# Trainium2: a decoder block's start, its third attention dilation, one split of gate weights and the first merge

## The chip, the cores and the metric

The kernel runs on one core of one Trainium2 chip. Its engines are TensorE (PE in the profile; PEld is its weight load), VectorE (DVE), ScalarE (ACT), GpSimd (POOL) and SyncE (SP), which here only issues DMAs. The metric is the device time of one execution in microseconds, the median of several. The arithmetic is fp32, kept by products of three: each operand is split into a high part (rounded to the type fp32r) and a low part, and high x high, high x low and low x high are summed in PSUM.

## The reference

For 2048 tokens of width 1024:

```python
h = rmsnorm(x, norm_pre_mix)
proj = h @ w_in                      # 1024 x 5376
q, k = rope(proj[:, :768]), rope(proj[:, 768:1536]); v = proj[:, 1536:2304]
u, z = gelu(proj[:, 2304:2816]), gelu(proj[:, 2816:3328])
gate_a, gate_b = sigmoid(proj[:, 3328:4352]), sigmoid(proj[:, 4352:])
y_attn = attention(q, k, v)          # 12 heads of 64 in 3 groups; dilations 1, 4, 16, window of 129 keys
y_gmlp = u * (tril(w_spatial) @ layernorm(z) + b_spatial)     # per chunk of 128 tokens
y = (gate_a * (y_attn @ w_branch_attn) + gate_b * (y_gmlp @ w_branch_gmlp)) @ w_out
x = x + rmsnorm(y, norm_post_mix)
h = rmsnorm(x, norm_pre_mlp)
x = x + rmsnorm(relu(h @ w_mlp_in) ** 2 @ w_mlp_out, norm_post_mlp)
```

A token t of a dilation d belongs to residue t mod d; within a residue the attention is a plain causal band, worked in blocks of 128.

## The kernel before

The kernel runs in stages over four chunks (c = 0 to 3) of 512 tokens, each of four blocks of 128.

*Values, queries, keys.* A block of x is loaded (`load_x`), normalised with the gain `gpre` (`prenorm_rows`), transposed by TensorE and split into `hT` (`prenorm_cols`, which also keeps a copy `hr` for DRAM, `hTd`). `v_block` multiplies it by the value weights: `va` for dilations 1 and 4, `vb` for the third. The weights of the first blocks, raws 0 to 2, are loaded by `early_load` and split on several engines by `early_split`. Six fp32 matmuls on a tile of ones (`busy`) stand ahead. `qk_pair` then projects queries and keys, rotates them (`t1`, `t2` on VectorE, `r` on POOL, L287 to L293), and stores high and low parts in DRAM (`qk_d`). For the dilations 4 and 16 the rotation's last step also reorders the tokens: for 4, by residue. For 16, `r` holds four groups of residues, and in a group (length index, residue) stand interleaved, so that a residue's elements are four apart.

*Attention and gates.* An attention unit handles one head and 512 tokens: loads of `kp` and `qq` (L546, L551) two units ahead, scores (L580 for the third dilation, L583 and L584 for the others), softmax on VectorE and ScalarE, transposes (L627), the value products (L646), and a sum `o` on VectorE (L653). Between its steps TensorE computes other columns of the projection: `filler` runs through u, z and the 16 pairs of gate columns, whose weights `w_g` are loaded one ahead by `load_w`: two raw halves, high parts on POOL (L72), low parts on VectorE or POOL (L78). When its first half of tokens is done, `reload_h` fetches `hT` of the other chunks from DRAM and splits it on POOL. The gates go to DRAM (`gate_d`).

*Merge.* For each chunk, in the order 2, 3, 0, 1, and for each of eight blocks of columns dt, `merge` loads two gates, takes their sigmoid on ScalarE, multiplies them by the branch products (L813), adds (L815) and splits the sum for the product with w_out. Meanwhile, in the first merge, `spatial_out` works off the last spatial products and loads and splits one eighth of w_out (`load_wo`) per dt. `out_block` multiplies by w_out, normalises, adds x and normalises again for the MLP. After that come the MLP's two products, which the change doesn't touch.

*What sets the order.* TensorE runs in the order of the program text. The instructions of the other engines and of SyncE's queue are put in order by a planner that follows the data; inside `as_written()` those too run in the order of the text, and `behind()` makes later ones follow the last one so far. Every engine runs its list in order: a waiting instruction holds up the ones behind it.

## Time and profile before

| | |
|---|---|
| median of 3 runs | 2757.62 us (2757.6 to 2757.78) |
| the profiled execution's own time | 2753.64 us |
| its span | 2751.9 us |
| mean granted TensorE clock | 0.994 |
| TensorE busy | 2699.0 us, 98% |
| VectorE, ScalarE, POOL busy | 57%, 38%, 35% |
| DMA moved | 426.00 MB, 155 GB/s |

A row of the timeline has the start and the length in us, the engine, the line, the operation, out<-in and the count; in brackets stands the idle time ahead of it and what ended that. In a row of a group stand the count, the busy time in us and the mean in ns of one. TensorE's matmuls are pipelined, so the distance between two starts is shorter than one's length.

### The profile page before, as it was taken

How to read it: one execution, taken by the hardware profiler on the slowest of the kernel's cores; microseconds unless marked ns; L12 is line 12 of the kernel's file. 1: busy time of each engine (PE TensorE's matmuls, PEld its weight loads, DVE VectorE, ACT ScalarE, POOL GpSimd, SP SyncE). 2: the span in 40 equal slices, each digit the busy share in tenths (PEclk: the TensorE clock that was granted, in tenths of full speed). 3: DMA queues.
4: the chain of work that ended last, by engine and by line, in shares of the span. 5: the costliest groups of instructions: out<-in, count | busy, mean ns of one | idle time of the engine just before them, and what ended most of it. 6: DMA issues, size and time to landing. Idle time of an engine off the chain costs nothing. (4 is left out here: it accounts for less than half of the span.)

```text
span 2751.9 us, 34711 instructions
## 1 busy us (share of the span) xinstructions
PE 2699.0 (98%) x12668; PEld 2237.4 (81%) x12668; DVE 1558.8 (57%) x2646; ACT 1050.3 (38%) x2145; POOL 965.5 (35%) x782
## 2 busy tenths in 40 slices
PE   8999999999999999999999999999999999999998
PEld 7888888888888888787787788878887888888887
DVE  5655552344343345555556644655436878888866
ACT  5213111244444322344444544555544332233334
POOL 0351341200140013302215432223214766676645
PEclk9999999999999999999999999999999999999999
DMA  7445446366676645555658433554343122222236
GB/s 266 171 146 172 153 143 211 112 195 196 192 222 200 194 159 176 184 191 161 184 168 287 154 106 124 181 171 119 111 138 122 52 87 85 84 85 85 87 107 213
DMA packets 298380, 426.00 MB, mean 155 GB/s; under 512 B 18528, under 2 KB 172384, under 8 KB 298208
## 3 DMA queue, kind: packets, MB, share of 16 engines
q1 hardware_dynamic: 206672, 370.28, 41.6%
q10 hardware_dynamic: 91536, 53.49, 6.5%
q8 instruction: 100, 1.64, 0.2%
q14 instruction: 72, 0.59, 0.1%
HBM read 282.99 MB, written 140.71 MB: 154 GB/s over the span
## 5 line engine op out<-in xcount | busy, mean ns | idle before, releaser
L1558 PE MATMUL ya<-T_spots,s 128*128 128x512 f32 x1176 | 291.6, 391 | 3.3 <-DVE acc L1566 3.3
L1558 PEld LDWEIGHTS ya<-T_spots,s 128*128 128x128 f32 x1176 | 220.7, 188 | 52.3 <-ACT T_spots L70 3.1
L70 ACT ACTIVATE s<-sraw 128x768 fp32r<-128x768 f32 (+1 forms) x184 | 127.4, 696 | 337.5 <-POOL sraw L1355 150.0
L1016 PE MATMUL aa<-B,A 128*128 128x512 f32 x768 | 186.9, 395 | 8.5 <-ACT xs L1030 7.7
L78 DVE TENSOR_TENSOR s<-sraw,s 128x512 fp32r<-128x512 f32 x171 | 179.6, 1075 | 7.1 <-ACT s L70 7.0
L987 POOL TENSOR_TENSOR s<-w1r 128x512 f32<-128x512 f32 x32 | 42.3, 1322 | 396.6 <-DVE S L78 337.9
L1016 PEld LDWEIGHTS aa<-B,A 128*128 128x128 f32 x768 | 145.0, 190 | 43.1 <-ACT xs L1030 9.0
L1558 PE MATMUL yc<-T_spots,s 128*128 128x512 f32 x624 | 160.8, 391 | 0.0
L72 POOL TENSOR_SCALAR w_g<-w_g_r 128x1024 fp32r<-128x1024 f32 x32 | 34.1, 1081 | 354.3 <-PE g L97 292.8
L95 PE MATMUL x<-hT_a,wq 128*128 128x512 f32 x384 | 149.7, 390 | 0.0
L97 PE MATMUL x<-hT_a,wq 128*128 128x512 f32 x384 | 149.5, 389 | 0.0
L96 PE MATMUL x<-hT_a,wq 128*128 128x512 f32 x384 | 149.4, 389 | 0.0
L653 DVE TENSOR_REDUCE o<-po 128x256 f32<-128x512 f32 x48 | 33.1, 690 | 194.4 <-PE po L652 194.4
L1558 PEld LDWEIGHTS yc<-T_spots,s 128*128 128x128 f32 x624 | 117.2, 188 | 25.6
L70 ACT ACTIVATE hl<-r 128x512 fp32r<-128x512 f32 x48 | 30.4, 633 | 233.2 <-POOL r L287 89.0
L78 POOL TENSOR_TENSOR T_spots<-w2r,T_spots 128x512 fp32r<-128x512 f32 x70 | 104.6, 1521 | 7.5 <-ACT T_spots L70 7.5
L95 PE MATMUL o<-wo,mg 128*128 128x512 f32 x256 | 101.5, 396 | 5.1 <-ACT mg L70 4.6
L95 PE MATMUL g<-hT_b,w_g 128*128 128x512 f32 x256 | 105.6, 412 | 0.0
L815 POOL TENSOR_TENSOR g<-g,g 128x512 f32<-128x512 f32 x28 | 38.8, 1385 | 187.4 <-DVE g L813 187.2
L95 PE MATMUL g<-hT_a,w_g 128*128 128x512 f32 x256 | 104.3, 407 | 0.0
L1354 POOL TENSOR_TENSOR sraw<-sraw 128x256 f32<-128x256 f32 x56 | 41.4, 739 | 178.4 <-DVE s L78 164.1
L70 ACT ACTIVATE S<-w1r 128x512 fp32r<-128x512 f32 x96 | 60.0, 629 | 114.2 <-PE ac L1016 69.3
(380 smaller groups left out, 7272.2 us busy)
## 6 DMA issues: line engine op xcount, KB each, us to landing
w1r<-in_w_mlp_in_dram SPq DMA_DIRECT2D x64, 512.0 KB, 3.5
sraw<-sd SPq DMA_DIRECT2D x128, 256.0 KB, 3.4
qk<-hl SPq DMA_DIRECT2D x24, 1024.0 KB, 5.3
qq<-qk SPq DMA_DIRECT2D x96, 256.0 KB, 5.0
w_g_r<-in_w_in_dram SPq DMA_DIRECT2D x32, 512.0 KB, 5.0
gated<-gt SPq DMA_DIRECT2D x64, 256.0 KB, 3.3
g<-gated SPq DMA_DIRECT2D x64, 256.0 KB, 4.3
sd<-u ACTq DMA_DIRECT2D x64, 256.0 KB, 2.8
```

Of the source, the lines that this page charges most:

```text
L70: act.activation(hi, src, AF.Copy)
L72: pool.tensor_scalar(hi, src, 1.0, 1.0, op0=OP.mult, op1=OP.mult)
L78: (pool if lo_eng == "pool" else dve).tensor_sub(lo, src, f32(hi))
L95: pe.matmul(ps, lh, rh, start=start, stop=False)
L96: pe.matmul(ps, lh, rl, start=False, stop=False)
L97: pe.matmul(ps, ll, rh, start=False, stop=stop)
L653: dve.tensor_reduce(ot[:, :, j * 64:(j + 1) * 64], po.rearrange("p (b h e) -> p b e h", b=4, h=2), axis=AX.X, op=OP.add)
L815: (dve if dt == KT - 1 else pool).tensor_add(parts[0], parts[0], parts[1])
L987: pool.tensor_add(s1, a21, a22)
L1016: pe.matmul(p, w[:, l, k, :], h[:, r, k, :], start=i in (1, 6, 5) and not k and not n, stop=k == 3 and n == 2, skip_group_check=True)
L1354: pool.tensor_add(a22, a21, a22)
L1558: pe.matmul(p, s[:, l], w[r], start=i in (1, 2, 5) and not m and not o, stop=m == 1 and o == 2, skip_group_check=True)
```

## The change

Four things change.

1. *Start.* The gain row (4 KB) is loaded to one partition of a zeroed tile and spread to 128 partitions by two fp32 matmuls with ones, into two PSUM banks from which the first block is normalised; ScalarE copies them to `gpre` later. Before, one DMA spread it (512 KB). There are five busy matmuls ahead of the spread and two behind. The high parts of the first weights are all ScalarE's and the low parts all VectorE's, in the order of the text, with the copies `hr` of the first block last.
2. *First merge.* `early_gates` asks for eleven gates ahead of the merge, six in places that are used later by `xr`, `gpost` and `gmlp`, with the first two w_out loads between; w_out is loaded two eighths ahead. All adds L815 are VectorE's. In the other merges the loads of the next `yt` stand behind the first out block.
3. *Third dilation.* The rotation writes each residue contiguously, `kp` is loaded as four pieces (one residue each, four runs of 32 elements per row), and the product reads queries of a residue contiguously and keys in runs of 32.
4. *Gate weights.* With half 0, POOL takes the low parts of the third weight in place of those of the first two.

On VectorE at the start, where `raw_126`, `raw_127`, `raw_128` are the three weight raws, before:

```order
L192 SCALAR_TENSOR_TENSOR x_122<-x_122,r_pre_146,gpre 128x512 x2
L78 TENSOR_TENSOR wv_1_130<-raw_126,wv_1_130 128x4x256
L78 TENSOR_TENSOR wv_0_129<-raw_126,wv_0_129 128x4x256
L206 TENSOR_TENSOR hT_a_161<-pt_162,hT_a_161 128x4x128
L206 TENSOR_TENSOR hT_a_161<-pt_172,hT_a_161 128x4x128
L189 TENSOR_TENSOR ss_182<-ss_182 128x1
```

and in the changed kernel, with raws 130 to 132:

```order
L203 SCALAR_TENSOR_TENSOR x_127<-x_127,r_pre_152,gpre_124 128x512
L385 TENSOR_TENSOR wv_0_133<-raw_130,wv_0_133 128x4x256
L218 TENSOR_TENSOR hT_a_169<-pt_170,hT_a_169 128x4x128
L218 TENSOR_TENSOR hT_a_169<-pt_177,hT_a_169 128x4x128
L385 TENSOR_TENSOR wv_1_134<-raw_130,wv_1_134 128x4x256
L385 TENSOR_TENSOR wv_0_133<-raw_131,wv_0_133 128x4x256
L385 TENSOR_TENSOR wv_1_134<-raw_131,wv_1_134 128x4x256
L200 TENSOR_TENSOR ss_191<-ss_191 128x1
```

One low part now stands behind the split of `hT`, and both of the second raw stand ahead of the second block's normalisation.

ScalarE a little later, where `x_308` is the third block, before:

```order
L205 ACTIVATE hT_a_161<-pt_269 128x4x128
L188 ACTIVATE junk_311,ss_310<-x_308 128x512
L188 ACTIVATE junk_313,ss_310<-x_308 128x512
L209 ACTIVATE hr_266<-pt_259 128x512
L209 ACTIVATE hr_276<-pt_269 128x512
L102 ACTIVATE r_pre_316<-ss_310,edge 128x1
L322 ACTIVATE vt_208<-vb_210 128x4x64
```

and now, where it is `x_320`:

```order
L342 ACTIVATE vt_220<-va_221 128x8x64
L199 ACTIVATE junk_323,ss_322<-x_320 128x512
L199 ACTIVATE junk_325,ss_322<-x_320 128x512
L229 ACTIVATE hr_278<-pt_271 128x512
L229 ACTIVATE hr_288<-pt_281 128x512
L342 ACTIVATE vt_220<-vb_222 128x4x64
L102 ACTIVATE r_pre_328<-ss_322,edge 128x1
```

The root for the third block has moved behind the copy of `vb`.

SyncE's queue at the first merge (`g_20` is a gate of chunk 2, dt 0), before:

```order
L91 DMA yt_9506<-ygd 128x512
L795 DMA g_20_9526<-gated 128x512
L795 DMA g_20_9537<-gated 128x512
L91 DMA woraw_9601<-in_w_out_dram 128x1024
L795 DMA g_21_9605<-gated 128x512
L795 DMA g_21_9616<-gated 128x512
```

and now:

```order
L863 DMA gates_9583<-gated 128x512 x2
L839 DMA woraw_9588<-in_w_out_dram 128x1024
L863 DMA gates_9584<-gated 128x512 x2
L839 DMA woraw_9592<-in_w_out_dram 128x1024
L863 DMA gates_9585<-gated 128x512 x2
L872 DMA g_23_9596<-gated 128x512
L872 DMA g_23_9598<-gated 128x512
```

The loads are the same; the gates stand further ahead of their use.

POOL at the third gate weight of half 0 (`w_g_6903`, now `w_g_6915`), before:

```order
L72 TENSOR_SCALAR w_g_6903<-w_g_r_6904 128x1024
L72 TENSOR_SCALAR w_g_6903<-w_g_r_6908 128x1024
L72 TENSOR_SCALAR hT_b_6538<-hT_b_6538 128x1024
L78 TENSOR_TENSOR hT_b_6538<-hT_b_6538 128x1024
L72 TENSOR_SCALAR hT_b_6538<-hT_b_6538 128x1024
```

and now:

```order
L72 TENSOR_SCALAR w_g_6915<-w_g_r_6916 128x1024
L72 TENSOR_SCALAR w_g_6915<-w_g_r_6920 128x1024
L78 TENSOR_TENSOR w_g_6915<-w_g_r_6916,w_g_6915 128x1024
L78 TENSOR_TENSOR w_g_6915<-w_g_r_6920,w_g_6915 128x1024
L72 TENSOR_SCALAR hT_b_6550<-hT_b_6550 128x1024
```

Two low parts now stand between the high parts and the split of `hT_b`.

The diff, cut:

```diff
-    def prenorm_rows(c, i):
+    def prenorm_rows(c, i, gs=None):
...
-        for sl in cuts(c, i):
-            dve.scalar_tensor_tensor(xt[:, sl], xt[:, sl], r, gpre[:, sl], op0=OP.mult, op1=OP.mult)
+        for n, sl in enumerate(cuts(c, i)):
+            dve.scalar_tensor_tensor(xt[:, sl], xt[:, sl], r, gs[n] if gs else gpre[:, sl], op0=OP.mult, op1=OP.mult)
...
+            kept.append((k, p3))
+            if (c, i) != (0, 0):
+                keep_cols(c, i, kept)
+        return kept
+    def keep_cols(c, i, kept):
+        while kept:
+            k, p3 = kept.pop(0)
...
-                pool.tensor_tensor(r.rearrange("p (m l r) -> p m l r", m=4, r=4),
-                                   t1.rearrange("p (l m r) -> p m l r", m=4, r=4),
-                                   t2.rearrange("p (l m r) -> p m l r", m=4, r=4), op=op)
+                pool.tensor_tensor(r.rearrange("p (m r l) -> p m r l", m=4, r=4),
+                                   t1.rearrange("p (l m r) -> p m r l", m=4, r=4),
+                                   t2.rearrange("p (l m r) -> p m r l", m=4, r=4), op=op)
...
-        act.dma_start(gpre, bcast(a["norm_pre_mix"]))
+        rp = stack(e1a, "rp", 1, side="right")
+        row = rp.tile([P, D], F32, name="row", tag="rope", bufs=2)
+        busy = rp.tile([P, 256], F32, name="busy", tag="t1", bufs=2)
+        pool.memset(row, 0.0)
+        dve.memset(busy, 1.0)
-        rp = stack(e1a, "rp", 1, side="right")
-        busy = rp.tile([P, 256], F32, name="busy", tag="t1", bufs=2)
-        dve.memset(busy, 1.0)
+        act.dma_start(row[0:1], a["norm_pre_mix"])
+        act.dma_start(ident, a["ident"])
+        p = psum_aux("busy")
+        for _ in range(5):
+            pe.matmul(p[:, :256], busy[:, :P], busy, start=True, stop=True)
+        gp = [psum_mm(f"gpre{n}") for n in range(2)]
-            p = psum_aux(f"busy{n}")
-            for _ in range(3):
-                pe.matmul(p[:, :256], busy[:, :P], busy, start=True, stop=True)
+            pe.matmul(gp[n], busy[:, :P], row[:, n * 512:(n + 1) * 512], start=True, stop=True)
         load_x(0, 0)
-        sp.dma_start(ident, a["ident"])
         raws = [rp.tile([P, 2, 4, 256], F32, name=f"raw{g}", tag=t, bufs=2) for g, t in enumerate(("hl", "hl", "vt"))]
                 sp.dma_start(raws[g][:, kk], w_src(6 + g, kk))
-        def early_split(g, *engs):
-            for kk in range(2):
-                w = part(wide0[kk], g) if g < 2 else third0[:, kk]
-                split(w[:, 0], w[:, 1], raws[g][:, kk], *engs[kk])
-        early_load(0)
-        load_x(0, 1)
-        early_load(1)
-        early_load(2)
-        prenorm_rows(0, 0)
-        early_split(0, ("pool", "dve"), ("act", "dve"))
-        prenorm_cols(0, 0)
-        prenorm_rows(0, 1)
-        early_split(1, ("act", "pool"), ("act", "dve"))
-        early_split(2, ("act", "dve"), ("pool", "dve"))
+        def early(g, kk):
+            w = part(wide0[kk], g) if g < 2 else third0[:, kk]
+            return w[:, 0], w[:, 1], raws[g][:, kk]
+        def hi(g, kk):
+            w = early(g, kk)
+            act.activation(w[0], w[2], AF.Copy)
+        def lo(g, kk, eng):
+            w = early(g, kk)
+            eng.tensor_sub(w[1], w[2], f32(w[0]))
+        with as_written():
+            early_load(0)
+            load_x(0, 1)
+            early_load(1)
+            early_load(2)
+            prenorm_rows(0, 0, gp)
+            p = psum_aux("busy")
+            for _ in range(2):
+                pe.matmul(p[:, :256], busy[:, :P], busy, start=True, stop=True)
+            hi(0, 0)
+            hi(0, 1)
+            lo(0, 0, dve)
+            kept = prenorm_cols(0, 0)
+            lo(0, 1, dve)
+            hi(1, 0)
+            hi(1, 1)
+            lo(1, 0, dve)
+            lo(1, 1, dve)
+            for n in range(2):
+                act.activation(gpre[:, n * 512:(n + 1) * 512], gp[n], AF.Copy)
+            prenorm_rows(0, 1)
+            hi(2, 0)
+            hi(2, 1)
+            lo(2, 0, dve)
+            lo(2, 1, dve)
+            keep_cols(0, 0, kept)
+        first = behind()
...
-                loaded[q] = load_w(wi, f"w_{kind}{n}{half}", "pool" if (kind, half) == ("g", 0) and n < 2 else "dve")
+                loaded[q] = load_w(wi, f"w_{kind}{n}{half}", "pool" if (kind, half) == ("g", 0) and n == 2 else "dve")
...
-        sp.dma_start(f32(kp)[:, :nkb * P], qk_d[g][one][j * P:(j + 1) * P, k0:k0 + nkb * P])
+        rows = qk_d[g][one][j * P:(j + 1) * P, k0:k0 + nkb * P]
+        if g == 2:
+            for r in range(4):
+                sp.dma_start(f32(kp)[:, r * P:(r + 1) * P].rearrange("p (c l) -> p c l", c=4),
+                             rows.rearrange("p (c r l) -> p r c l", c=4, r=4)[:, r])
+        else:
+            sp.dma_start(f32(kp)[:, :nkb * P], rows)
...
-                    pe.matmul(o.rearrange("p (h k) -> p h k", h=2), kp[:, b:512:4], qq[:, :, b::4],
-                              start=True, stop=True)
+                    pe.matmul(o.rearrange("p (h c l) -> p h c l", h=2, c=4), kp[:, b * P:(b + 1) * P],
+                              qq.rearrange("p h (c r l) -> p r h c l", c=4, r=4)[:, b], start=True, stop=True)
...
+    wo_raw = {}
     def load_wo(k):
-        raw = bot.tile([P, D], F32, name=f"woraw{k}", tag="y1", bufs=2)
-        split_in(wo[k], a["w_out"][:, k, :], raw, "act")
+        wo_raw[k] = bot.tile([P, D], F32, name=f"woraw{k}", tag="y1", bufs=2)
+        sp.dma_start(wo_raw[k], a["w_out"][:, k, :])
+    def split_wo(k):
+        split(wo[k][:, 0], wo[k][:, 1], wo_raw.pop(k))
+        if k + 2 < KT:
+            load_wo(k + 2)
...
+    def early_gates(c):
+        w = [bot.tile([P, D], F32, name=f"gates{n}", tag=t) for n, t in enumerate(("xr", "gpost", "gmlp"))]
+        places = [z[:, h * 512:(h + 1) * 512] for z in w for h in range(2)]
+        for n in range(11):
+            dt, wch = n // 2, n % 2
+            if n < 6:
+                gates[c, dt, wch] = places[n]
+                sp.dma_start(places[n], gate_d[wch * 8 + dt, :, c * 512:(c + 1) * 512])
+            else:
+                load_gate(c, dt, wch)
+            if n in (1, 3):
+                load_wo(n // 2)
...
-            (dve if dt == KT - 1 else pool).tensor_add(parts[0], parts[0], parts[1])
+            dve.tensor_add(parts[0], parts[0], parts[1])
...
-        load_wo(dt)
+        split_wo(dt)
...
+    early_gates(2)
...
-        if n < 3:
-            yt = load_y(chunks[n + 1])
-            for dt in range(2):
-                for wch in range(2):
-                    load_gate(chunks[n + 1], dt, wch)
...
+            if n < 3 and not i:
+                yt = load_y(chunks[n + 1])
+                for dt in range(2):
+                    for wch in range(2):
+                        load_gate(chunks[n + 1], dt, wch)
```

More of the change, by code (lines that the diff above doesn't have):

```diff
@@ L164, in block_kernel, with as_written, behind @@
     st = stack(e1, "st", 2)
+    def as_written():
+        t = mybir.EngineType
+        return tc.manual_schedule(engines={t.Activation, t.DVE, t.Pool, t.SP})
+    def behind():
+        es, t = ExitStack(), mybir.EngineType
+        for e in (t.Activation, t.DVE, t.Pool, t.SP):
+            es.enter_context(tc.issue_after(next(i for i in reversed(nc.cur_bb.bb.instructions) if i.engine == e)))
+        return es
     hT = {}
@@ L198, in prenorm_cols @@
         h, xt = hT[c], xts.pop((c, i))
+        kept = []
         for k in range(0, KT, 4):
@@ L380, in block_kernel @@
                 v_block(rp, wv, c, i, between)
+                if (c, i) == (0, 1):
+                    first.close()
             nxt = load_w(0, f"wq00{half}")
@@ L771, in block_kernel @@
     sm = stack(e2b, "sm2", 2)
[L772 to L773 removed]
+    gpost = gmlp = None
     gtp = stack(e2, "gtp", 2)
@@ L1088, in spatial_out @@
     def spatial_out(dt):
-        nonlocal ttp
+        nonlocal ttp, gpost, gmlp
         if dt < 2:
@@ L1096, in spatial_out @@
             ttp = stack(e2r, "ttp", 2, side="right")
-        load_wo(dt)
+        split_wo(dt)
         if dt == KT - 1:
+            gpost = bot.tile([P, D], F32, name="gpost")
+            gmlp = bot.tile([P, D], F32, name="gmlp")
             sp.dma_start(gpost, bcast(a["norm_post_mix"]))
@@ L1140, in block_kernel @@
                     lone_a(1, q, n_, raw.rearrange("p (k c) -> p k c", k=4))
-    def as_written():
-        t = mybir.EngineType
-        return tc.manual_schedule(engines={t.Activation, t.DVE, t.Pool, t.SP})
-    def behind():
-        es, t = ExitStack(), mybir.EngineType
-        for e in (t.Activation, t.DVE, t.Pool, t.SP):
-            es.enter_context(tc.issue_after(next(i for i in reversed(nc.cur_bb.bb.instructions) if i.engine == e)))
-        return es
     first_half, second_half = 1, 0
```

2 lines of the change are left out of this document (removed).

## The prediction

> **What bounds the kernel.** I read the page's first part, then TensorE's waits grouped by releaser, then the timeline at each of them. In a row of the waits stand the total, the count and the longest, in us.
>
> ```profile
> span 2751.9 us, 34711 instructions
> PE 2699.0 (98%) x12668; PEld 2237.4 (81%) x12668; DVE 1558.8 (57%) x2646; ACT 1050.3 (38%) x2145; POOL 965.5 (35%) x782
> ```
> ```profile
> ...
> PE b L95 <- DVE g L813: 5.0, 4, 1.7
> PE o L95 <- ACT mg L70: 4.6, 4, 1.9
> PE pT L627 <- DVE o L653: 4.1, 2, 3.4
> ...
> PE pt L868 <- DVE y L862: 3.4, 1, 3.4
> ```
>
> TensorE is busy for 98% of the span, so time is saved only where it stands still or where a busy matmul is slower than it need be. The second kind isn't in the list of waits. The sum below is made against the profiled execution's 2753.64 us (span 2751.9); the median of the runs is 2757.62, 4.0 more, so I add 4.0 at the end. What can be told from no change is 0.2%, 5.5 us.
>
> **A, the start.**
>
> ```profile
> 1.31 5.46 PE L339 MATMUL busy<-busy 128*128 128x256 f32 x12 [1.31 <-DVE busy L335]
> 10.32 1.94 PE L202 MATMUL pt<-ident,x 128*128 128x128 f32 x8 [3.55 <-DVE x L192]
> ...
> 15.81 0.42 PE L96 MATMUL va<-wv,hT_a 128*128 128x256 f32 x1
> ...
> 17.11 0.28 PE L97 MATMUL va<-wv,hT_a 128*128 128x256 f32 x1
> ...
> 21.09 0.39 PE L96 MATMUL va<-wv,hT_a 128*128 128x256 f32 x1 [1.43 <-DVE wv L78]
> ...
> 26.26 0.40 PE L95 MATMUL va<-wv,hT_a 128*128 128x512 f32 x1
> ```
> ```profile
> 6.61 0.60 ACT L188 ACTIVATE junk<-x 128x512 f32<-128x512 f32 x1 [0.71 <-DMA x<-in_x_dram]
> ```
> ```profile
> 8.72 2.16 DVE L192 SCALAR_TENSOR_TENSOR x<-x,r_pre,gpre 128x512 f32<-128x512 f32 x2
> 10.93 2.36 DVE L78 TENSOR_TENSOR wv<-raw,wv 128x1024 fp32r<-128x1024 f32 x2
> ```
> ```profile
> 15.14 2.42 POOL L78 TENSOR_TENSOR wv<-raw,wv 128x1024 fp32r<-128x1024 f32 x1 [5.46 <-ACT wv L70]
> ```
>
> (Start, length, engine, line; in brackets the idle time before and what ended it.) The busy matmuls end at 6.77, the first transposes come at 10.32, and va's matmuls take 0.42 us at 15.81 and 0.28 at 17.11: the clock was half until then. VectorE's normalisation at 8.72 goes back to ScalarE's second square at 6.61, which waited for x's DMA. The change takes 512 KB (gpre spread to 128 rows) out of the queues ahead of x, so I let x land 1 to 2 us earlier and the normalisation start at about 7.1. Two matmuls that spread the gain and two more busy ones fill TensorE until then (two passes each of 5.46/12 = 0.455 us, more for the 512 wide ones: to about 8.9), so the clock stays up. Then va's 48 matmuls run at the short length, and group 1 no longer stands behind POOL's 2.42 us low part (VectorE's is 2.36/2 = 1.18): the 1.43 at 21.09 goes too. I put group 1's end near 16.8 and vb's near 22.2, where va of the next block begins at 26.26 now: 4 us. Part is given back. In ScalarE's new order the third block's r_pre stands behind vb's copy (before, ahead of it), so that block's transposes come an estimated 1.4 us late. I take 2.5, with 0 to 4 as ends: nothing if x's landing isn't set by gpre. POOL's memset of the row (128x1024) and two gain copies on ScalarE are new; ScalarE's idle time there covers the copies, the memset runs beside x's load.
>
> **B, the first merge, and the adds.**
>
> ```profile
> 1119.45 0.80 SPq L795 DMA_DIRECT2D g<-gated  x2
> ```
> ```profile
> 1125.83 1.28 DVE L813 TENSOR_TENSOR g<-g,b 128x512 f32<-128x512 f32 x2 [1.21 <-ACT g L809]
> 1175.16 0.69 DVE L815 TENSOR_TENSOR g<-g,g 128x512 f32<-128x512 f32 x1
> ```
> ```profile
> 850.00:900.00 50.00, 49.93 (x260) 42.94 (x260) 20.05 (x78) 19.71 (x67) 2.07 (x2) 1.00 0.69 214
> 900.00:950.00 50.00, 50.00 (x264) 43.24 (x263) 18.81 (x65) 17.59 (x57) 4.12 (x4) 1.00 0.60 185
> 950.00:1000.00 50.00, 50.00 (x262) 42.96 (x262) 14.92 (x63) 18.34 (x58) 2.06 (x2) 1.00 0.32 108
> ...
> 1119.30:1168.10 48.80, 42.50 (x209) 33.54 (x207) 33.04 (x50) 22.11 (x32) 15.16 (x10) 1.00 0.76 235
> ```
> ```profile
> L815 POOL TENSOR_TENSOR g<-g,g 128x512 f32<-128x512 f32 x28 | 38.8, 1385 | 187.4 <-DVE g L813 187.2 <-DVE r_pm L105 0.2
> ```
>
> The third of these fences is the busy time of stretches: from and to, length, then PE, weight loads, VectorE, ScalarE, POOL, the granted clock, DMA's share and GB/s. In the last stretch, the first merge's products, TensorE stands still for 48.80 - 42.50 = 6.3 us at full clock, most of it the 5.0 on the gates; about 1.4 of the 4.6 on the last parts (L95 o) follow in the out block behind it: 7.7. The first gate isn't asked for until 1119.45, and from then on gate, sigmoid, product, POOL's add (1.385 us) and ScalarE's and VectorE's split run as a chain through two or three buffers. In the change two gates are asked for ahead of that time and nine right at it, and the add takes 0.69 on VectorE in place of 1.385 plus a handover. What is late next is VectorE: it is busy for 33.0 us of the stretch, seven more adds make it 33.0 + 7 x 0.69 = 37.8, and the stretch shrinks towards 42.5, so its queue holds up a product here and there. I let 1 of the 7.7 stay and take 6.7, ends 3 (VectorE sets the pace) and 7.7. On SyncE the first wo load waits for a place that z's products read until 1119, as the first gate did, and holds nine gates behind it; at 0.40 an issue (0.80 for two) all are out within 5 us. The cover is the two gates ahead of it, which feed the first product.
>
> The later merges' adds also move: 24 x (1.385 - 0.69) off their chains, 0.69 more on VectorE each. Their longest stall, 3.4 at y (L862), has two adds and a split ahead of it on VectorE, with less beside them on POOL. I take nothing, with 1.5 either way. Moving the loads of yt behind the first out block leaves them hidden under that block's products.
>
> **C, the third dilation.**
>
> ```profile
> L580 PE MATMUL s<-qq,kp 128*128 128x256 f32 x64 | 20.6, 460 | 0.0
> ```
> ```profile
> 742.29 0.29 PE L583 MATMUL s<-kp,qq 128*128 128x256 f32 x1
> 742.42 0.28 PE L584 MATMUL s<-kp,qq 128*128 128x256 f32 x1
> ...
> 849.55 1.29 PE L580 MATMUL s<-qq,kp 128*128 128x256 f32 x4
> 850.66 0.41 PE L95 MATMUL g<-hT_b,w_g 128*128 128x512 f32 x1
> 859.23 1.29 PE L580 MATMUL s<-qq,kp 128*128 128x256 f32 x4
> ```
> ```profile
> q1 hardware_dynamic: 206672, 370.28, 41.6%
> q10 hardware_dynamic: 91536, 53.49, 6.5%
> ```
> ```profile
> 842.71 0.58 SPq L546 DMA_DIRECT2D kp<-qk  x1
> ```
> ```profile
> L289 POOL TENSOR_TENSOR r<-t,t 128x512 f32<-128x512 f32 x16 | 36.2, 2273 | 19.2 <-DVE t L284 19.2
> L293 POOL TENSOR_TENSOR r<-t,t 128x512 f32<-128x512 f32 x16 | 22.3, 1406 | 22.9 <-DVE t L284 19.3 <-DVE ss L189 3.6
> ```
>
> At L580 queries and keys are read at every fourth element, and a matmul takes 460 ns; one of the same shape on contiguous operands (742.29, an earlier dilation) takes 280 to 290. Four of L580 hold TensorE from 849.55 to 850.66, 1.11 us; the contiguous ones come 0.13 apart, 0.52 for four. TensorE is full in those stretches (49.93 and 50.00 of 50), so each of 16 units is 0.59 shorter: 9.5 us.
>
> The price is kp's load: 128 runs of 2 KB become 2048 of 128 bytes, in four DMAs. From the page's queues a q10 packet of 584 bytes took 6.5% x 16 x 2751.9 / 91536 = 31 ns and a q1 packet of 1792 bytes 89. The line through both gives 9 ns at 128 bytes; no gain from being smaller gives 31. A unit now takes 9.68 us (849.55 to 859.23), its DMA work 0.69 x 9.68 = 6.7, and 2.4 us are free in the new 9.1. kp's packets take 128 x t per engine against about 0.8 now: at 20 ns, between the ends, 1.8 more, which is hidden; at 31 ns 3.2 more, which costs 0.8 in each of the five units of the first window and nothing in the later ones (0.60): 4 us. SyncE's issue grows from 0.58 to 2.3 of 9 us. The rotation before it (L293) now gathers with a step of 16 elements: 1.4 us becomes at least the 2.27 of L289's four-step gather, 16 x 0.87 = 14 us on POOL, under TensorE's projections, which never wait for it (no row in the list). I take 9, ends 4 and 10.
>
> **D, the gate weights' low parts.**
>
> ```profile
> 784.98 0.48 PE L627 MATMUL pT<-ident,e 128*128 128x128 f32 x1 [3.44 <-DVE o L653]
> ...
> 786.53 0.63 PE L97 MATMUL g<-hT_b,w_g 128*128 128x512 f32 x1
> ...
> 788.24 0.40 PE L95 MATMUL g<-hT_b,w_g 128*128 128x512 f32 x1
> ```
> ```profile
> 780.29 4.04 DVE L78 TENSOR_TENSOR w_g<-w_g_r,w_g 128x1024 fp32r<-128x1024 f32 x2 [4.79 <-POOL w_g L72]
> ```
> ```profile
> 745.99 4.76 POOL L78 TENSOR_TENSOR w_g<-w_g_r,w_g 128x1024 fp32r<-128x1024 f32 x2
> ```
>
> VectorE's low parts of the third gate weight, slowed beside POOL's work to 4.04 for two, run to 784.3 and hold up the reduction behind them (L653), and with it TensorE's transposes: 3.44, and then matmuls of 0.63 until 788.24, where 0.40 is usual. From 784.98 on that is 3.3 us at half pace, 1.6 lost. Both go: 5.0. The two weights before it come to VectorE without POOL beside them (2.36 for two, as at 10.93); an attention step behind them can wait for that, up to 0.5 each. On POOL the third weight's 4.76 now stands ahead of the second half of hT_b's splits; I put their results level with TensorE's need, so a stall of up to 1 can come there. I take 4.5, ends 2.5 and 5.0.
>
> **Sum.** 2.5 + 6.7 + 9 + 4.5 = 22.7. 2753.6 - 22.7 = 2730.9 profiled, 2735 in the median.
>
> **Rivals.**
> 1. Slower: kp's small packets bind the third dilation. At 62 ns, twice q10's, kp takes 7.1 us more per unit: ten units become 6.2 + 7.1 = 13.3 against 9.1, six later ones at a share near 0.32 10.2; 42 + 7 = 49 more than in my sum, 2784. It outweighs the rest from about 47 ns, where ten units lose 2.4 each. For it speaks that 2048 runs replace 128; against, that q10's 584-byte packets took half that. By the Trainium skill ("DMA: Bandwidth & Descriptors", Specifications) line rate needs at least 512 bytes and smaller transfers are read, modified and written; it would make 128-byte runs dearer than my line, and no row here shows one by itself.
> 2. The reads stay slow: 32-element runs on the keys' side or the matmul itself set the pace, and only the weight load speeds up. C gives 0 to 4, the rest 13.7: 2742. Against it stands that the contiguous rows at 742 are fast on both sides, and 32 elements is a long run. By the Trainium skill ("SBUF — State Buffer", Specifications) a 16-byte line has to be hit at least twice for full bandwidth; a step of four fp32 hits it once, a run of 32 four times, and by that the full 9.5 comes, not this rival. The rows at 460 and 290 agree as far as they go.
> 3. The first merge becomes VectorE's: each wo split and add ahead of a gate product is paid for, B gives 3: 2739.
> 4. The start isn't shortened, since the third block's transposes or a half clock take its place: 2737.5.
>
> **How the numbers follow.** My forecast with rivals 3 and 4, alone or together, within 2728 to 2743: 0.74. Rival 2: 0.10. A milder rival 1 (31 to 45 ns), 2739 to 2755: 0.07. Rival 1 in full, or another stall of over 25 us: 0.09. The line of no difference runs from 2752.1 to 2763.1: faster 0.88, same 0.04, slower 0.08. The range takes in the ends of the terms: best 4 + 7.7 + 1.5 + 10 + 5 = 28 (2729.5), worst 0 + 3 - 1.5 + 4 + 2.5 = 8 (2749.6, 2750); below it reaches 4 us further, since a half clock that is spared elsewhere isn't in the sum. The likeliest case's own range is 2728 to 2743.
>
> **What would show it.** Right: pt at about 9, va's second group without a wait, vb's end at 22 to 23; the first gates loaded before 1119 and no add on POOL; the third dilation's products at some 300 ns a matmul and 0.52 for four, DMA share under 0.85 there; no 3.4 us wait of transposes on the reduction, and none above 1 us at the gates' products on hT_b. Wrong: waits of the third dilation on qq or kp by DMA, a matmul there near 460, VectorE's products of the first merge behind wo splits, or a new half clock where a wait of over 3 us appears.

## The result, and the profile after

| | before | changed |
|---|---|---|
| median of the runs | 2757.61 us (2754.89 to 2760.83, 6 runs) | 2734.34 us (2729.40 to 2737.85, 6 runs) |
| ratio | | 0.9916, 95% interval 0.9903 to 0.9928 |
| the profiled execution | 2753.64 us | 2733.0 us |
| its span | 2751.9 us | 2731.3 us |

The change is faster by 0.84%, 23 us; the prediction was 2735. The page's first part and its small packets after the change:

```profile
span 2731.3 us, 34716 instructions
...
PE 2688.8 (98%) x12674; PEld 2230.0 (82%) x12674; DVE 1583.9 (58%) x2677; ACT 1054.8 (39%) x2149; POOL 929.5 (34%) x750
...
q1 hardware_dynamic: 238016, 370.22, 43.2%
```

TensorE's waits by releaser, after:

```profile
PE pt L945 <- DVE y L939: 5.3, 1, 5.3
...
PE sz L480 <- DVE sb L487: 1.9, 1, 1.9
PE va L95 <- ACT hT_a L217: 1.8, 1, 1.8
...
PE o L95 <- ACT mg L70: 1.6, 2, 1.2
...
PE pT L683 <- DVE o L709: 1.3, 2, 0.7
PE o L95 <- DVE g L890: 1.2, 1, 1.2
PE pt L214 <- DVE x L203: 1.0, 2, 0.5
```

The waits on the gates (5.0) and the one of 3.4 at the transposes pT are gone. New is the 1.8 at the start, on ScalarE's copy of the first block. The one at the spatial products (sz) has grown from 0.9 to 1.9, and the one on y from 3.4 to 5.3.

Where the time went is seen best by stages. Each number below is the distance between the starts of the same two TensorE instructions in each run's one profile: "start" until the third block's transposes (29.16 before); "third weight" from 743.0 to the value products at 791.0 of before; "dilation 16" from there to 986.5; "merge 1" from its first product (1119.26) to the first transposes behind its out block (1197.4); "merges 2-4" from there to 1369.1, the transposes after the fourth merge.

| run | start | third weight | dilation 16 | merge 1 | merges 2-4 |
|---|---|---|---|---|---|
| before | 29.2 | 48.0 | 195.5 | 78.1 | 171.7 |
| changed | 26.8 | 43.1 | 187.5 | 73.2 | 172.6 |
| e1, start as before | 29.5 | 43.1 | 187.9 | 74.5 | 174.2 |
| e2, merges as before | 26.5 | 43.1 | 187.5 | 77.0 | 171.2 |
| e3, queries alone contiguous | 26.5 | 43.1 | 193.9 | 74.0 | 173.3 |
| e4, keys alone in runs | 25.6 | 43.1 | 194.0 | 75.1 | 173.8 |
| e5, three weights on POOL | 27.4 | 42.8 | 187.5 | 74.0 | 173.4 |
| e6, adds on POOL | 26.2 | 43.1 | 187.3 | 71.7 | 173.4 |
| e7, small loads twice, early | 27.1 | 43.1 | 187.4 | 76.6 | 174.5 |
| e8, eight gates | 25.9 | 43.1 | 187.3 | 72.2 | 171.7 |
| e9, weights as before | 26.1 | 47.6 | 187.4 | 74.8 | 174.0 |
| e10, gain by DMA | 26.8 | 43.1 | 187.4 | 75.1 | 173.3 |
| e11, small loads twice, in place | 25.8 | 43.1 | 210.8 | 71.8 | 174.2 |
| e12, eight gates, other start order | 27.6 | 43.1 | 187.5 | 71.1 | 173.9 |

Of the 20.6 us of span between before and changed, 2.4 came from the start, 4.9 from the third weight, 8.1 from the third dilation, 4.9 from the first merge, and 0.9 was lost in the later merges. Another 1.4 lies behind 1369.1 (1382.84 us to the end before, 1381.47 after), in the last out blocks and the MLP; there the runs take 1380.3 to 1384.0, so that this is scatter and no gain. The two middle columns repeat to a few tenths over runs with the same code there. The start and the merges don't. With the changed kernel's start (changed, e2 to e9, e11) the start takes 25.6 to 27.4, mean 26.4; with that of before (before, e1) 29.2 and 29.5. With the changed kernel's merges (changed, e1, e3, e4, e5, e7, e9, e10, e11) merge 1 takes 71.8 to 76.6, mean 74.3, and the later ones 172.6 to 174.5, mean 173.7.

### The profile page after: what moved, and what is told of

The parts are those of the page before. It is cut to its first block, busy times and chain, and to the rows that moved or that the text cites. A ratio compares the mean times of both kernels' runs of the same rounds, so it can differ in the third digit from the quotient of the medians.

```text
span 2731.3 us, 34716 instructions
## 1 busy us (share of the span) xinstructions
PE 2688.8 (98%) x12674; PEld 2230.0 (82%) x12674; DVE 1583.9 (58%) x2677; ACT 1054.8 (39%) x2149; POOL 929.5 (34%) x750
## 3 DMA queue, kind: packets, MB, share of 16 engines
q1 hardware_dynamic: 238016, 370.22, 43.2%
## 5 line engine op out<-in xcount | busy, mean ns | idle before, releaser
L95 PE MATMUL o<-wo,mg 128*128 128x512 f32 x256 | 100.7, 393 | 2.8 <-ACT mg L70 1.6
L97 PE MATMUL o<-wo,mg 128*128 128x512 f32 x256 | 100.0, 391 | 0.5 <-DVE mg L78 0.4
```

What stands on the lines that cost most here:

```text
L95: pe.matmul(ps, lh, rh, start=start, stop=False)
L97: pe.matmul(ps, ll, rh, start=False, stop=stop)
```

## The experiments

Each starts from the changed kernel. The "before" that shared their chips had medians of 2755.01 (e1 to e4), 2754.46 (e5 to e8) and 2754.69 (e9 to e12), where the changed kernel's own had 2757.61. So a difference of 3 us between the medians of two of these kernels is no larger than that between these befores; each ratio is to the before that shared the chip.

**e1: the start as before.**

```diff
-        act.dma_start(row[0:1], a["norm_pre_mix"])
+        act.dma_start(gpre, bcast(a["norm_pre_mix"]))
...
-            prenorm_rows(0, 0, gp)
+        prenorm_rows(0, 0)
+        early_split(0, ("pool", "dve"), ("act", "dve"))
...
```

> The changed kernel with the start of before (gain spread by one DMA, weights split on several engines); the rest as changed. In the changed kernel's profile the third block's transposes come at 26.76 instead of 29.16. If that 2.4 us stays all the way and touches nothing else, this run takes 2.4 us more than the changed kernel, and every later landmark is 2.4 us later. The rival, that a stall further on absorbs a start that comes later, gives 0 to 1.

2738.32 us, ratio to before 0.9937 (0.9922 to 0.9952). The third block starts at 29.51, 2.75 later, and nothing behind it absorbs that. What else this run has over the changed one's profile (its merges) is within what equal code shows. By the means of the stage, 29.3 against 26.4, the start gains about 3.

**e10: the start's order as changed, the gain by one DMA.**

```diff
-        act.dma_start(row[0:1], a["norm_pre_mix"])
+        act.dma_start(gpre, bcast(a["norm_pre_mix"]))
...
-            prenorm_rows(0, 0, gp)
+            prenorm_rows(0, 0)
...
-            for n in range(2):
-                act.activation(gpre[:, n * 512:(n + 1) * 512], gp[n], AF.Copy)
```

> The changed start, its written order and its busy matmuls, but the gain is spread to 128 rows by one DMA of 512 KB, as before, and the first block is normalised from that. If the 512 KB ahead of x make x land late, ScalarE's second square starts 1.2 to 1.7 us later than in the changed kernel (at 6.1 to 6.6 in place of 4.93), the first transposes wait for it, and about half of the 2.4 us is lost. If the written order alone brought the gain, the second square still comes late, but the third block's transposes come within 0.5 us of 26.76.

2733.70 us, 0.9922 (0.9909 to 0.9936). ScalarE's second square, in the changed kernel and here, and the third block's transposes here:

```profile
4.93 0.60 ACT L199 ACTIVATE junk<-x 128x512 f32<-128x512 f32 x1 [0.26 <-DMA x<-in_x_dram]
```
```profile
6.76 0.60 ACT L199 ACTIVATE junk<-x 128x512 f32<-128x512 f32 x1 [0.60 <-DMA x<-in_x_dram]
```
```profile
26.81 1.06 PE L214 MATMUL pt<-ident,x 128*128 128x128 f32 x8 [0.52 <-DVE x L203]
```

The 512 KB do hold x up, by 1.8 us. But the third block comes at 26.81 against 26.76, and against the mean of 26.4: some 0.4 of the start's 3, within its scatter, is that of norm_pre_mix's new way in. The rest is that of the written order, the splits' engines, the busy matmuls and the loads ahead of x, which no run takes apart. In the changed kernel:

```profile
19.42 1.06 PE L214 MATMUL pt<-ident,x 128*128 128x128 f32 x8 [0.49 <-DVE x L203]
...
26.76 1.07 PE L214 MATMUL pt<-ident,x 128*128 128x128 f32 x8 [0.53 <-DVE x L203]
```

At the second block's transposes TensorE waits for VectorE's normalised x in every run with the changed start: 0.5 here, 0.8 in e10, 1.1 to 1.9 in the others. So a first block that comes earlier ends in that wait.

**e12: eight gates, and the second high part behind the first block's copy.**

```diff
             hi(0, 0)
-            hi(0, 1)
             lo(0, 0, dve)
             kept = prenorm_cols(0, 0)
+            hi(0, 1)
...
-        for n in range(11):
+        for n in range(8):
```

> Eight early gates as in the run that was 4 us faster than the changed kernel, and at the start the high part of the second half of the first weight behind the first block's copy on ScalarE, not ahead of it. In the changed kernel TensorE waits 1.83 us at 11.11 for that copy, which stands behind the high part from 9.52 to 10.48. If this wait is ScalarE's order alone, it falls to about 0.7 and the run takes 1 us less than the eight gates alone: about 2729. If the weight's own landing holds TensorE next, nothing is gained: 2730.

2733.30 us (5 runs), 0.9919 (0.9906 to 0.9933). In the changed kernel and here:

```profile
9.52 1.06 ACT L381 ACTIVATE wv<-raw 128x1024 fp32r<-128x1024 f32 x1 [0.21 <-DMA raw<-in_w_in_dram]
10.48 1.07 ACT L217 ACTIVATE hT_a<-pt 128x512 fp32r<-128x512 f32 x2
```
```profile
9.33 1.09 ACT L217 ACTIVATE hT_a<-pt 128x512 fp32r<-128x512 f32 x2 [0.99 <-PE pt L214]
```

The copy comes 1.15 earlier, and the third block's transposes at 27.60, not earlier. TensorE's wait ahead of va is 0.25 here where it was 1.83, but it is 0.25 to 1.16 in the nine other runs with the changed start as well, so the 1.83 wasn't ScalarE's order alone. What ends the start are the chains of the second block (a wait of 1.9 on VectorE's x here) and of the third (0.3). Besides, 2.0 us are lost at one unit's transposes near 550, where TensorE waits for ScalarE; no other run has that. Nothing is gained, so this version isn't a better one.

**e9: the gate weights' low parts as before.**

```diff
-                loaded[q] = load_w(wi, f"w_{kind}{n}{half}", "pool" if (kind, half) == ("g", 0) and n == 2 else "dve")
+                loaded[q] = load_w(wi, f"w_{kind}{n}{half}", "pool" if (kind, half) == ("g", 0) and n < 2 else "dve")
```

> The changed kernel with the low parts of the gate weights as before: the first two of half 0 on POOL, the third on VectorE. If these cost what the two profiles show between the third weight and the value products behind it (5.95 + 1.26 - 2.40 = 4.8 us), the wait of TensorE's transposes on the reduction is back at 3 to 3.5, the matmuls behind it run at half the clock for some us, and the run is about 5 us slower than the changed kernel (2739). If the earlier start alone moved the clash of POOL and VectorE, the wait comes out at 1 or less and the run equals the changed kernel.

2737.90 us, 0.9939 (0.9925 to 0.9953). TensorE's waits and VectorE's row here:

```profile
PE pT L683 <- DVE o L709: 4.4, 3, 3.1
```
```profile
776.92 4.02 DVE L78 TENSOR_TENSOR w_g<-w_g_r,w_g 128x1024 fp32r<-128x1024 f32 x2 [4.28 <-POOL w_g L72]
```

The low parts take 4.02 again, the longest wait is 3.1, and the stage is 47.6 where it was 43.1. The earlier start doesn't move the clash.

**e5: all three low parts on POOL.**

```diff
-                loaded[q] = load_w(wi, f"w_{kind}{n}{half}", "pool" if (kind, half) == ("g", 0) and n == 2 else "dve")
+                loaded[q] = load_w(wi, f"w_{kind}{n}{half}", "pool" if (kind, half) == ("g", 0) and n < 3 else "dve")
```

> Low parts of all three first gate weights of half 0 on POOL; the changed kernel has only the third there, before had only the first two. If the gain of 4.8 us is the third weight's alone and the first two cost VectorE next to nothing in either place, this run equals the changed kernel within 1 us and its transposes behind the reduction wait as little. If taking the first two off POOL is what keeps the split of hT_b in time, a wait of 1 to 5 us on hT_b comes at the gates' products near 785.

2734.68 us, 0.9929 (0.9914 to 0.9944); the stage takes 42.8. The gain is the third weight's move alone (0.3 apart at most), and no wait on hT_b's split appears. In the changed kernel POOL does it like this:

```profile
778.85 4.75 POOL L78 TENSOR_TENSOR w_g<-w_g_r,w_g 128x1024 fp32r<-128x1024 f32 x2
783.55 1.06 POOL L72 TENSOR_SCALAR hT_b<-hT_b 128x1024 fp32r<-128x1024 f32 x1
```

**e3 and e4: one side of the third dilation's products at a time.** e3:

```diff
+                if which == 0:
                     pool.tensor_tensor(r.rearrange("p (m r l) -> p m r l", m=4, r=4),
...
+                else:
+                    pool.tensor_tensor(r.rearrange("p (m l r) -> p m l r", m=4, r=4),
...
...
-                              qq.rearrange("p h (c r l) -> p r h c l", c=4, r=4)[:, b], start=True, stop=True)
+                              qq[:, :, b::4], start=True, stop=True)
```

> Third dilation: only the queries (the stationary side) are contiguous per residue and loaded in four pieces; the keys are stored as before and read at every fourth element. Before, four products took 1.11 us with the weight loads at 328 ns and the matmuls at 460; changed, 0.56 at 304. If the strided weight load set the pace, the products fall to about 0.56 for four here and the run equals the changed kernel. If the strided moving operand set it, they stay near 1.1 and the run is 8 to 9 us slower than the changed one. If each costs on its own, something between, 0.8.

e4 has `which == 1` there, `kp[:, b:512:4]` for the queries, and one load of them.

> The other half: keys are stored per residue and read in runs of 32, queries as before, loaded whole in one DMA of 2 KB rows and read at every fourth element. If the strided weight load set the pace, four products still take about 1.1 us and the run is 8 to 9 us slower than the changed one. If the moving operand set it, they fall to about 0.56, the run equals the changed kernel, and the four small loads of queries are not needed. If each costs on its own, 0.8.

e3 2739.04 us, 0.9939 (0.9922 to 0.9956); e4 2740.89 us, 0.9945 (0.9931 to 0.9960). The groups (matmul and weight load; busy us, mean ns) in the changed kernel (first an earlier dilation's contiguous products, then this one's), in e3 and in e4:

```profile
L639 PE MATMUL s<-kp,qq 128*128 128x256 f32 x128 | 34.3, 302 | 0.0
...
L636 PE MATMUL s<-qq,kp 128*128 128x256 f32 x64 | 11.6, 304 | 0.0
```
```profile
L641 PE MATMUL s<-qq,kp 128*128 128x256 f32 x64 | 18.7, 440 | 0.0
...
L641 PEld LDWEIGHTS s<-qq,kp 128*128 128x128 f32 x64 | 11.5, 200 | 0.7
```
```profile
L636 PE MATMUL s<-qq,kp 128*128 128x256 f32 x64 | 19.0, 419 | 0.0
...
L636 PEld LDWEIGHTS s<-qq,kp 128*128 128x128 f32 x64 | 16.2, 326 | 0.0
```

Four products take, from their start to the next matmul's:

```profile
842.37 0.73 PE L636 MATMUL s<-qq,kp 128*128 128x256 f32 x4
842.93 0.39 PE L95 MATMUL g<-hT_b,w_g 128*128 128x512 f32 x1
```
```profile
842.30 1.17 PE L641 MATMUL s<-qq,kp 128*128 128x256 f32 x4
843.28 0.43 PE L95 MATMUL g<-hT_b,w_g 128*128 128x512 f32 x1
```
```profile
841.10 1.19 PE L636 MATMUL s<-qq,kp 128*128 128x256 f32 x4
842.13 0.39 PE L95 MATMUL g<-hT_b,w_g 128*128 128x512 f32 x1
```

0.56 with both, 0.98 and 1.03 with one, 1.11 with none. None of the three expectations holds: neither side is the one, and the sides don't add. Either strided side alone keeps the pace near the slow one. That would fit a weight load that runs beside the matmul of the product before it, where the slower of the two sets the distance; no run shows this overlap by itself. Of the stage's 8.1 us one side alone brings 1.6.

**e7: the queries' small loads twice.**

```diff
+            again = at1.tile([P, 512], F32, name=f"again_{nm}", tag="again", bufs=2)
+            for r in range(4):
+                sp.dma_start(again[:, r * P:(r + 1) * P].rearrange("p (c l) -> p c l", c=4),
+                             rows.rearrange("p (c r l) -> p r c l", c=4, r=4)[:, r])
```

> The queries' four small loads of each unit of the third dilation are issued a second time, into a tile that nobody reads: 2048 more runs of 128 bytes per unit. A unit now takes 8.45 us and its DMA work is 0.81 x 8.45 = 6.8. At 22 ns per small packet (from the two pages: q1's share and packets) the second set adds 2.8 us: 9.6, so the ten units of the busy stretch each lose about 1.2 us, 12 in all, and TensorE waits for qq or kp. At 31 ns it adds 4.0: 24 lost. At 9 ns it adds 1.2 and nothing is lost.

2736.11 us, 0.9930 (0.9913 to 0.9946). This missed its place. The second set waits for nothing, and the planner issued all of it early (columns: count, shortest, median and longest ns, first and last start in us):

```profile
L603 SPq DMA_DIRECT2D again<-qk x64: 359/507/2978, 457.3 to 504.7; - x64
```

It says nothing on the third dilation, but it gives a price: q1 has 33,792 packets more, and 44.0% of 16 x 2739.4 against 43.2% of 16 x 2731.3 is 406 us more, 12 ns each. Equal packets differ by up to 138 us in this total between runs, 4 ns each, so the packet records are the better source: in the changed kernel's trace the 32,768 packets of 128 bytes take 13 ns each, where the median of 512 bytes is 28 and that of 2048 bytes 84.

**e11: the same, in buffers shared with the queries.**

```diff
-        kp = at1.tile([P, 5 * P], F32R, name=f"kp_{nm}", tag="akp", bufs=4)
+        kp = at1.tile([P, 5 * P], F32R, name=f"kp_{nm}", tag="akp", bufs=7)
...
+            again = at1.tile([P, 5 * P], F32R, name=f"again_{nm}", tag="akp", bufs=7)
```

> The second set of the queries' small loads again, now in buffers that the queries' tiles share, so that each comes at its unit and not before the stage. At 22 to 31 ns per packet of 128 bytes a unit's DMA work of 6.8 us becomes 9.6 to 10.8 against 8.45, and 12 to 24 us are lost. The second set in the run before cost the q1 queue 0.8% of 16 engines for 33,792 packets, some 10 ns each; by that it adds 1.3 and nothing is lost: the third dilation's units stay at 8.45.

2757.13 us (10 runs), 1.0011 (1.0002 to 1.0020): 23 us slower than the changed kernel, the number of the packet theory, but not by its way. TensorE's longest wait, and the rows of VectorE and SyncE behind it:

```profile
PE pv L706 <- DVE o L713: 19.1, 1, 19.1
```
```profile
960.50 1.23 DVE L78 TENSOR_TENSOR w_g<-w_g_r,w_g 128x1024 fp32r<-128x1024 f32 x1 [23.98 <-POOL w_g L72]
```
```profile
952.16 0.59 SPq L603 DMA_DIRECT2D again<-qk  x1
952.86 0.45 SPq L91 DMA_DIRECT2D w_g_r<-in_w_in_dram  x1
```

Until 942 the units nearly keep their pace (the stage is 1.3 us behind at the gate product, 845.17 in the changed kernel and 845.50 here, and 0.2 more follow until then). Then one wait of 19.1 takes most of it: SyncE's queue, with four issues more per unit, had fallen behind, and a gate weight was asked for only at 952.86, behind the second set; its low part stands at the head of VectorE's list, and the attention step's reduction behind it. In this run the packets cost 43.8% of 16 x 2755.9 less 18,879, 434 us for the same number, 13 ns. So the packets' price isn't what binds; SyncE's queue is, with one set more. Part of its delay is this run's own making: its issues for kp stood five times, 8.0 us in all, until a second set had landed in a shared buffer, and the run doesn't tell this from the time of the added issues.

**e2: the merges as before.**

```diff
-    early_gates(2)
...
-            dve.tensor_add(parts[0], parts[0], parts[1])
+            (dve if dt == KT - 1 else pool).tensor_add(parts[0], parts[0], parts[1])
...
-        split_wo(dt)
+        load_wo(dt)
...
+        if n < 3:
+            yt = load_y(chunks[n + 1])
...
```

> The changed kernel with the merges of before (gates asked for in the merge, adds on POOL, w_out one eighth ahead, yt loaded ahead of the out blocks). By the two profiles the first merge and its out blocks gain 4.9 us net of a new wait of 1.85 at the spatial products, and the later merges give 1 back. If those belong to this part, this run is about 4 us slower than the changed kernel (2738), the first merge's waits on the gates are back at about 5, and the wait of 5.3 on y is back near 3.4. If the later loss isn't this part's, the run is 5 slower and the 5.3 stays.

2738.15 us, 0.9938 (0.9923 to 0.9953), 3.8 above the changed kernel. Merge 1 takes 77.0, and merges 2 to 4 take 171.2, less than with the changed kernel's merges in any run (e8 comes close with 171.7). The waits on the gates and on y:

```profile
PE b L95 <- DVE g L869: 5.0, 5, 1.8
...
PE pt L924 <- DVE y L918: 3.4, 1, 3.4
```

The expectation's first case holds: the first merge gains, the later ones lose, and the loss is this part's. But the stages don't carry the 3.8: the four merges take 248.2 together, where the changed kernel's take 245.8 in its profile and 248.0 by the mean of equal code, and 2.5 of what this profile takes longer lies behind them, where the scatter of equal code is 3.7 (1380.3 to 1384.0).

**e6: the adds on POOL.**

```diff
-            dve.tensor_add(parts[0], parts[0], parts[1])
+            (dve if dt == KT - 1 else pool).tensor_add(parts[0], parts[0], parts[1])
```

> The changed kernel with the merges' adds on POOL again (all but the last of each merge), gates early as changed. If the early gates carry the first merge's gain, the first out block starts no more than 1 us later against the merge's start than in the changed kernel. If the adds carry it (1.385 us each plus a handover on the chain), it starts 3 or more later. In the later merges, the wait of 5.3 on y falls back to 3.4 or less if the adds on VectorE caused the 1.9 more; it stays at about 5 if they didn't.

2733.22 us, 0.9924 (0.9909 to 0.9939). Merge 1 takes 71.7, no longer than with the adds on VectorE: what is asked for early carries that gain. That it is the gates and not the earlier loads of w_out is argued from the waits on the gates, 5.0 in e2 and none here; no run takes the two apart. Waits here:

```profile
PE pt L945 <- ACT mg L70: 3.4, 1, 3.4
...
PE sz L480 <- DVE sb L487: 3.2, 1, 3.2
```

The wait of these transposes is back at 3.4 (put down to ScalarE's mg now), yet merges 2 to 4 take 173.4, as with the changed code. The adds shift where the later merges wait; they aren't the 2 us lost there. Left are the loads of yt and the gates behind the first out block, which no run tells apart: that stays open.

**e8: eight gates ahead.**

```diff
-        for n in range(11):
+        for n in range(8):
```

> Eight gates are asked for ahead of the first merge instead of eleven. In the changed kernel five single gate loads take SyncE from 1107.12 to 1111.0, the store of the spatial products' first result comes behind them at 1112.99, and VectorE waits for that store's buffer until 1119.75, which makes the wait of 1.85 of TensorE at 1120.65. If SyncE's queue is the cause, three loads fewer bring the store 2 us forward and that wait falls to 0 or near it, with 1.5 to 2 us gained. If the buffers or the store's own time set it, the wait stays at 1 to 2; and the three gates, asked for late, may cost 1 us of their own at the products of dt 4 and 5.

2729.84 us (2728.67 to 2733.90), 0.9914 (0.9899 to 0.9929): against its own before it stands where the changed kernel stands (0.9916), so a faster kernel isn't shown. Nor is a faster stage: merge 1 takes 72.2 and, with e12, 71.1, but eleven gates take 71.7 to 76.6. The wait at sz is gone, and 3.2 on late gates has come:

```profile
PE b L95 <- DVE g L890: 3.2, 2, 1.6
```

But not by SyncE's queue. The store goes out at 1111.90 here and at 1112.99 in the changed kernel, where all is 1.08 later: the same. The difference is in the DMA engines. In the changed kernel, then here (busy times, clock, DMA share, GB/s):

```profile
1112.00:1120.00 8.00, 6.80 (x42) 5.82 (x40) 6.73 (x10) 5.95 (x10) 0.96 (x1) 1.00 1.00 333
```
```profile
1112.00:1120.00 8.00, 8.00 (x53) 7.14 (x52) 6.58 (x10) 2.64 (x5) 1.16 (x1) 1.00 0.72 239
```
```profile
1119.75 0.75 DVE L487 SCALAR_TENSOR_TENSOR sb<-sz,lngb,bsp 128x512 f32<-128x512 f32 x1 [1.23 <-DMA ygd<-sb]
```
```profile
1116.03 0.74 DVE L487 SCALAR_TENSOR_TENSOR sb<-sz,lngb,bsp 128x512 f32<-128x512 f32 x1
```

The landing of the stores from 1108 to 1122, two in the changed kernel (one landing is on record) and four here:

```profile
DMA to landing us min/median/max: 6.7/6.7/6.7
```
```profile
DMA to landing us min/median/max: 2.3/3.5/4.1
```

With eleven gates the engines are full (1.00; here it is 0.83 over the matching stretch, 1110.92 to 1118.92), the store of the first spatial result takes 6.7 us to land where it takes 3.9 here, and VectorE's next result waits for a buffer. The other runs agree: with eleven gates that store takes 6.4 to 7.7 and TensorE waits 1.5 to 3.2 at sz in each of ten; with eight, 3.9 and 3.3, and no such wait.

## Why the prediction was right, and where it wasn't

*A, the start: 2.5 said, 2.4 in the profile, 2.75 by e1.* The size was right, the reason wrong, and in the profile two errors offset each other: the next block's va comes 2.9 earlier (23.32 against 26.26) where 4 was worked out, and 0.5 is given back where 1.4 was estimated. The step "VectorE's normalisation at 8.72 goes back to ScalarE's second square at 6.61, which waited for x's DMA" led to the 512 KB as the lever. The square does come 1.7 earlier, but e10, without that, starts the third block at the same time. What ends the start are the second block's chain, which the working left out, and the part that I had booked as given back, the third block's; rival 4 was right on the place, not on the price. "So the clock stays up" failed in this profile:

```profile
11.11 0.39 PE L95 MATMUL va<-wv,hT_a 128*128 128x256 f32 x1 [1.83 <-ACT hT_a L217]
...
12.22 0.42 PE L95 MATMUL va<-wv,hT_a 128*128 128x256 f32 x1
```

The granted clock was 0.50 from 12.20 to 14.80, and 13 of va's matmuls took 0.41 or more, as 14 did before; that is a half clock of the kind that I had named as a sign of being wrong, at a wait of 1.8. In the eleven other runs with this order the wait was 0.25 to 1.16 and none of the first 48 of va's matmuls took 0.40 or more, so there the step held.

*B, the merges: 6.7 said for the first; 4.9 in the profile, 2.7 against e2 by the mean of equal code.* Two steps were mis-sized. "At 0.40 an issue all are out within 5 us" priced the nine gates by SyncE's time (all were out in 6.8, from 1104.18 to 1111.01); e8 shows that their transfers fill the DMA engines and hold up a store that TensorE waits for, 1.9 us. And the 0 for the later merges was 0.9 us too good in the profile, 2.5 against e2 by the mean, beyond the 1.5 allowed. The four merges together gain 4.0 in the profiles and 0.2 against e2 by the mean, so what this part is worth stays open. The add's shorter chain, named as part of the gain, brings nothing (e6). That VectorE sets the pace (rival 3) is seen in part: TensorE's one wait of 1.2 at the out block is on VectorE's product. It is 1.2 to 3.1 in all nine runs with eleven gates and the adds on VectorE, and absent in e6, with the adds on POOL.

*C, the third dilation: 9 said, 8.1 measured.* A unit is 0.56 shorter where 0.59 was worked out, and 0.9 is lost in all, nearly all of it at two places (0.57 at 844.86, 0.25 at 911.10). The unit of 9.68 us that the price was set against is the longest one; most take 9.01 before and 8.45 now, so that less time was free than the working says. The 128-byte runs cost 13 ns, between the ends of 9 and 31 and below the 20 taken, and no unit waits for them:

```profile
842.00:892.00 50.00, 49.37 (x276) 42.05 (x275) 20.32 (x78) 20.18 (x67) 2.08 (x3) 1.00 0.81 220
892.00:942.00 50.00, 49.92 (x278) 42.36 (x277) 20.37 (x76) 20.81 (x67) 4.12 (x4) 1.00 0.82 204
```

The DMA share rose from 0.69 and 0.60 to 0.81 and 0.82, TensorE stays full. Rival 1 is out at one set of small loads; e11 shows that twice as many take the change's whole gain, through SyncE's queue. The rule of the Trainium skill ("DMA: Bandwidth & Descriptors", Specifications) that line rate needs transfers of at least 512 bytes would have spoken for rival 1; in bytes per time the small ones do cost more (128 bytes in 13 ns against 512 in 28), but not enough to matter here. Rival 2 is out too: runs of 32 elements read as fast as contiguous operands, 304 ns against the earlier dilations' 302 in the same profile. That is what the Trainium skill ("SBUF — State Buffer", Specifications) gives for runs that hit a 16-byte line four times. The POOL gather was priced well, at least 2.27 us said and 2.22 measured:

```profile
L313 POOL TENSOR_TENSOR r<-t,t 128x512 f32<-128x512 f32 x16 | 35.4, 2224 | 19.6 <-DVE t L304 16.0 <-DVE ss L200 3.6
```

*D, the gate weights: 4.5 said, 4.9 measured,* 4.5 by e9. The stall of up to 1 us on hT_b didn't come, and the first two weights cost nothing in either place (e5).

The sum, 22.7, stands against 20.6 in the profiled executions and 23.3 in the medians. C and D, 13.5 of it, are borne out by their own stages. The median agreeing to 1 us is partly luck: the same kernel's runs span 8 us, and B's shortfall is made up by 1.4 of scatter behind the merges and by before's median, 3 us higher here than beside the experiments.

## What to carry to other kernels

When loads are asked for earlier, price their transfers and not only their issues: look in the stretch for a store or a load with a consumer close behind, and give the early loads only what the DMA engines have free. A matmul with two strided operands has to be mended on both sides, since either alone keeps most of the loss. And of a list worked in order ask what stands behind a load that comes late: in e11 one late weight cost 19 us through the low part at the head of VectorE's list.

## What was unexpected in the hardware

- One strided operand costs nearly as much as two: 0.98 and 1.03 us for four products against 1.11, and 0.56 with none. Both the weight load (200 against 326 ns) and the matmul slow down by themselves.
- A packet of 128 bytes took 13 ns, one of 512 bytes 28 and one of 2048 bytes 84 (medians of the changed kernel's trace). The prediction's 584 bytes in 31 ns were the mean of a mixed queue, mostly packets of 512.
- Equal code differs by up to 5 us between executions in merge 1 (71.8 to 76.6), while the stages between, where TensorE is full, repeat to a few tenths.
